# The second norm's scale and shift move behind the transposes, two token tiles at a time

## The chip, the core and the metric

The kernel runs on one core of a Trainium2 chip. Its engines are TensorE (PE in the rows, with its weight loads as PEld), VectorE (DVE), ScalarE (ACT) and GpSimd (POOL); SyncE (SP) issues most of the DMAs. The metric is the device time of one execution in microseconds (us), as the median of several timed runs.

## What is computed

One diffusion layer: 512 latent tokens and 256 context tokens of 1024 channels go through a mixer (linear attention and a state-space branch), and the latent tokens then through a feed-forward network. The change touches the place between the two:

```python
h_lat = h_lat + g1 * mix
h_lat = h_lat + g2 * _swiglu(modulate(rms_norm(h_lat, norm2_w), sh2, sc2), w_gate, w_up, w_down)

def rms_norm(x, w):        # y * w with y = x * rsqrt(mean(x*x) + EPS)
def modulate(h, shift, scale):
    return h * (1 + scale) + shift
```

`sh1, sc1, g1, sh2, sc2, g2` are the six parts of `silu(c) @ w_ada + b_ada`, so `sc2`, `sh2` and `norm2_w` hold one number for each channel and are the same for all tokens.

## The kernel before

All matrices are float32 and are multiplied in three passes: every operand is split into a high half (a rounded copy, made by ACT, line L188) and a low half (the rest, made by DVE or POOL, L189), and PE adds high x high, high x low and low x high (`mm3`, L204 to L206, for the row projections; L1067 to L1069 in the feed-forward network). Weights come in blocks of 512 KB through three `raw` buffers (L176, issued by SP) and are split into two buffers `whi` and two `wlo`.

Around the change the program runs as follows. The gates of the modulation (`ada`, a column for each of 48 blocks of 128 channels) are done while the mixer runs. Then `ada` is transposed, written to DRAM as rows (`adr`), and read back, spread over all 128 partitions: `g1r` (512 KB), `sh2` and `sc2` (two halves of 256 KB each) and `norm2_w` (`n2`, two halves), L949 to L963. DVE makes `sc2 = (1 + sc2) * n2` (L965).

Then comes the output projection. `merge(j)`, j from 0 to 7 (L980 to L991), loads two gate tiles `tgm_j_0` and `tgm_j_1` (and a third, `yam_j`, for j below 2) from DRAM into four buffers with the tag `E4`, and makes rows j of the operand on DVE (L988), POOL (L989), ACT (L990, high half) and DVE (L991, low half); each of these steps sets a buffer free for the loads of a later merge. The eight weight blocks `out_k` are multiplied with `g1r` on POOL (L187) and split. PE works through k = 0 to 3 for all tokens and then finishes k = 4 to 7 for one token tile `i` (128 tokens) after the other into the banks `ob[i][c]`.

For each token tile DVE adds the bank to `hres[i]` (L1022), ACT sums the squares (L1024), DVE and POOL make the factor `r` (L1027, L168, L170), and then

```python
nc.vector.scalar_tensor_tensor(xn, hres[i][...], r, sc2[half], ALU.mult, ALU.mult)     # L1031
(nc.gpsimd if (i, half) == (2, 1) else nc.vector).tensor_tensor(xn, xn, sh2[half], ALU.add)  # L1032
# L1035: four PE transposes of 128x128 into one PSUM bank
nc.scalar.activation(h2H[dst], pv, AF.Copy)                                            # L1038
nc.vector.tensor_tensor(h2L[dst], pv, h2H[dst].bitcast(F32), ALU.subtract)             # L1039
```

The feed-forward network begins with the weight blocks `gate` and `up` of j = 0 and 1 over tokens 0 to 255, then over tokens 256 to 511, so it needs tiles 0 and 1 first. From j = 2 on, `some_ada()` loads and sums one block of `w_ada` on POOL (L341 to L345) for the last gate `g2`, at every second j, eight blocks in all.

The order on each engine is set by a scheduler that plays the program on a timeline of its own; every engine then runs its list strictly in that order. Lines marked `tc.high_priority()` are put ahead.

## Time and profile before

| | |
|---|---|
| median of 3 runs | 1432.5 us (1431.48 to 1433.24) |
| the profiled execution's own time | 1428.55 us |
| its span from first to last instruction | 1426.7 us |
| busy PE, DVE, ACT, POOL | 95%, 62%, 35%, 33% of the span |
| DMA over the span | 175.49 MB moved, mean 123 GB/s |

The span is what the rows below are counted in; times in them are from its start. A busy share is a mean over stages with different limits, so the rows of single stretches tell more than the table. An idle time of an engine costs only where the work that ends last waits for it.

### The profile page before, as it was taken

Reading aid. Unit: us, or ns where it says so; the run is one execution under the profiler, and the core shown is the slowest. Engines: PE = TensorE matmul, PEld = TensorE weight load, DVE = VectorE, ACT = ScalarE, POOL = GpSimd, SP = SyncE. Lnnn points to the kernel's source line nnn. Section 1 sums busy time; section 2 is a strip of 40 time slices with the busy share of each in tenths; the row PEclk is TensorE's granted clock in tenths of the full one; section 3 lists DMA queues with packets and bytes.
Section 4 is the critical chain, followed back from the end, with each engine's and each line's share of the span. In section 5 each row is a group of like instructions: output and inputs, shape, how many; then the busy total and the mean of one; then the engine's idle time right before and its main releaser. Section 6 shows DMA issues by size and latency. Waiting matters only on the chain.

```text
span 1426.7 us, 19130 instructions
## 1 busy us (share of the span) xinstructions
PE 1349.4 (95%) x7462; PEld 1146.0 (80%) x7462; DVE 881.1 (62%) x1317; ACT 496.7 (35%) x825; POOL 476.1 (33%) x341
## 2 busy tenths in 40 slices
PE   5888999999998999998999989999889999999997
PEld 3687999889888778876887787778678888888886
DVE  4599757583595588558857975767683343433235
ACT  6464343433434132532332342332333323232222
POOL 1346555245423533343353324114641122100001
PEclk9998999999999999999999999999999999999999
DMA  9375433423422423323322333457423343333331
GB/s 370 123 259 151 128 102 111 126 93 126 122 75 67 141 98 101 97 73 90 104 82 89 96 97 101 158 184 267 135 87 109 113 122 115 120 116 93 100 106 72
DMA packets 71386, 175.49 MB, mean 123 GB/s; under 512 B 6384, under 2 KB 22912, under 8 KB 71168
## 3 DMA queue, kind: packets, MB, share of 16 engines
q1 hardware_dynamic: 57056, 161.11, 34.6%
q0 software_dynamic: 13952, 12.79, 3.8%
q8 instruction: 59, 0.97, 0.3%
q10 hardware_dynamic: 288, 0.36, 0.1%
...
## 4 chain that ended last, share of the span: by engine, by line
PE 66%; DVE 16%; DMA 9%; issue 5%; ACT 2%; POOL 1%; SPq 0%; POOLq 0%; DVEq 0%; ACTq 0%
DMA E<-cdr 6%; PE up L1069 3%; PE gate L1068 3%; PE gate L1069 3%; PE up L1068 3%; PE gate L1067 3%; PE up L1067 3%; DVE E L830 3%; PE db L204 3%; PE db L206 3%; PE db L205 3%; PE lv L577 2%; PE pb_pb L716 2%; PE pb_pb L715 2%; PE pb_pb L717 2%
## 5 line engine op out<-in xcount | busy, mean ns | idle before, releaser
L341 POOL TENSOR_TENSOR raw_ada<-raw_ada,cs 128x1024 f32<-128x1024 f32 x32 | 69.7, 2180 | 265.3 <-DMA raw_ada<-in_wts_dram 230.4
L830 DVE TENSOR_TENSOR E<-E,ebias 128x512 f32<-128x512 f32 x64 | 68.8, 1077 | 51.0 <-DMA E<-cdr 50.8
L343 POOL TENSOR_TENSOR raw_ada<-raw_ada 128x512 f32<-128x512 f32 x64 | 80.0, 1250 | 3.7
L386 PE MATMUL r_z<-whi_z,hH 128*128 128x256 f32 x256 | 74.6, 291 | 5.8 <-DVE z L781 3.0
L388 PE MATMUL r_z<-whi_z,hL 128*128 128x256 f32 x256 | 73.4, 287 | 0.0
L387 PE MATMUL r_z<-wlo_z,hH 128*128 128x256 f32 x256 | 73.0, 285 | 0.0
L1067 PE MATMUL gate<-h2H,whi_gate 128*128 128x512 f32 (+1 forms) x192 | 72.2, 376 | 0.0
L1068 PE MATMUL gate<-h2L,whi_gate 128*128 128x512 f32 (+1 forms) x192 | 72.1, 376 | 0.0
L1069 PE MATMUL gate<-h2H,wlo_gate 128*128 128x512 f32 (+1 forms) x192 | 71.9, 374 | 0.0
L189 POOL TENSOR_TENSOR wlo_xs<-raw_xs,whi_xs 128x1024 fp32r<-128x1024 f32 x16 | 40.6, 2536 | 75.3 <-ACT whi_xs L188 75.3
L1069 PE MATMUL up<-h2H,wlo_up 128*128 128x512 f32 x160 | 63.0, 394 | 0.0
L1068 PE MATMUL up<-h2L,whi_up 128*128 128x512 f32 x160 | 62.4, 390 | 0.0
L1067 PE MATMUL up<-h2H,whi_up 128*128 128x512 f32 x160 | 62.3, 389 | 0.0
L189 DVE TENSOR_TENSOR wlo_down<-raw_down,whi_down 128x1024 fp32r<-128x1024 f32 x18 | 22.1, 1225 | 62.4 <-ACT whi_down L188 62.3
L189 DVE TENSOR_TENSOR wlo_gate<-raw_gate,whi_gate 128x1024 fp32r<-128x1024 f32 x20 | 31.7, 1584 | 45.6 <-ACT whi_gate L188 45.6
L170 POOL TENSOR_TENSOR rr_f<-rv_f,negh 128x1 f32<-128x1 f32 x4 | 2.6, 662 | 168.5 <-DVE rv_f L168 168.5
L386 PE MATMUL r_v<-whi_v,hH 128*128 128x256 f32 x192 | 56.4, 294 | 0.0
L189 POOL TENSOR_TENSOR wlo_z<-raw_z,whi_z 128x1024 fp32r<-128x1024 f32 x16 | 39.6, 2475 | 49.2 <-ACT whi_z L188 36.6
L387 PE MATMUL r_v<-wlo_v,hH 128*128 128x256 f32 x192 | 55.5, 289 | 0.0
L715 PE MATMUL pb_pb<-yT,whi_pb 128*128 128x512 f32 x128 | 55.3, 434 | 0.0
L388 PE MATMUL r_v<-whi_v,hL 128*128 128x256 f32 x192 | 55.3, 288 | 0.0
L205 PE MATMUL db<-wlo_down,fH 128*128 128x512 f32 x142 | 55.3, 389 | 0.0
...
## 6 DMA issues: line engine op xcount, KB each, us to landing
...
```

Of the source, the lines that this page charges most:

```text
L189: (nc.gpsimd if split_pool[0] else nc.vector).tensor_tensor(lo, raw, hi.bitcast(F32), ALU.subtract)
L205: nc.tensor.matmul(out_, aH, bL, start=False, stop=False)
L341: nc.gpsimd.tensor_tensor(raw, raw, cs[:, :, 0:1].to_broadcast([P, KD, P]), ALU.mult)
L343: nc.gpsimd.tensor_tensor(raw[:, 0:n, :], raw[:, 0:n, :], raw[:, n:2 * n, :], ALU.add)
L386: nc.tensor.matmul(o, hH[:, kk, tk], hi[:, k, :], start=st, stop=False, skip_group_check=True)
L387: nc.tensor.matmul(o, hH[:, kk, tk], lo[:, k, :], start=False, stop=False, skip_group_check=True)
L388: nc.tensor.matmul(o, hL[:, kk, tk], hi[:, k, :], start=False, stop=sp, skip_group_check=True)
L715: nc.tensor.matmul(pt, hi[:, k, cl], aH[:, k, :], start=(k == 0), stop=False)
L830: nc.vector.tensor_tensor(ed, ed, ebias[:, d, n, hh].unsqueeze(2).to_broadcast([P, EH, P]), ALU.add)
L1067: nc.tensor.matmul(pts[kj][:, tk], hi[:, k, :], h2H[:, k, tk], start=(k == 0), stop=False)
L1068: nc.tensor.matmul(pts[kj][:, tk], hi[:, k, :], h2L[:, k, tk], start=False, stop=False)
L1069: nc.tensor.matmul(pts[kj][:, tk], lo[:, k, :], h2H[:, k, tk], start=False, stop=(k == KD - 1))
```

## The change

The scale and shift of the second norm are no longer rows spread over the partitions but columns, one number for each partition, used after the transposes, where the channels lie on partitions. The transposes therefore take `hres * r` alone, which ACT makes instead of DVE. Each PSUM bank now holds two blocks of 128 channels for two neighbouring token tiles, so that high and low halves are made for 256 tokens of one channel block at a time. The loads of `sh2`, `sc2` and `n2` and the two DVE steps on them are dropped, and only `g1` is written to DRAM. The last gate's blocks begin at j = 5 instead of 2.

```diff
-    adT = ch.tile([96, P], F32, tag="s2", name="adT", bufs=7)
+    adT = ch.tile([16, P], F32, tag="s2", name="adT", bufs=7)
...
-    sh2 = half_rows("sh2", 24)
-    sc2 = half_rows("sc2", 32)
-    for c in range(2):
-        n2 = ch.tile([P, 512], F32, tag="s2", name=f"n2_{c}", bufs=7)
-        nc.sync.dma_start(n2, rows[0:1, R_N2 + c * 512:R_N2 + (c + 1) * 512].to_broadcast([P, 512]))
-        nc.vector.scalar_tensor_tensor(sc2[c], sc2[c], 1.0, n2, ALU.add, ALU.mult)
+    s2c = cst.tile([P, KD], F32, name="s2c")
+    nc.vector.scalar_tensor_tensor(s2c, ada[:, 32:40, 0], 1.0, vecs[:, V_N2:V_N2 + KD], ALU.add, ALU.mult)
...
+        if i % 2 == 0:
+            pts = [sm_bank(f"hT_{i}_{q}") for q in range(4)]
         for half in range(2):
             xn = ch.tile([P, 512], F32, tag="z", name=f"hn_{i}_{half}", bufs=4)
-            nc.vector.scalar_tensor_tensor(xn, hres[i][:, half * 512:(half + 1) * 512], r, sc2[half], ALU.mult, ALU.mult)
-            (nc.gpsimd if (i, half) == (2, 1) else nc.vector).tensor_tensor(xn, xn, sh2[half], ALU.add)
-            pt = sm_bank(f"hT_{i}_{half}")
+            nc.scalar.activation(xn, hres[i][:, half * 512:(half + 1) * 512], AF.Copy, scale=r)
             for k in range(4):
-                nc.tensor.transpose(pt[:, k * P:(k + 1) * P], xn[:, k * P:(k + 1) * P], ident)
-            nc.scalar.activation(h2H[dst], pv, AF.Copy)
-            nc.vector.tensor_tensor(h2L[dst], pv, h2H[dst].bitcast(F32), ALU.subtract)
+                kk = half * 4 + k
+                c0 = (kk % 2) * 256 + (i % 2) * P
+                nc.tensor.transpose(pts[kk // 2][:, c0:c0 + P], xn[:, k * P:(k + 1) * P], ident)
+        if i % 2 == 1:
+            tk = slice((i - 1) * P, (i + 1) * P)
+            for k in range(KD):
+                pv = pts[k // 2][:, (k % 2) * 256:(k % 2) * 256 + 256]
+                sc, sh = s2c[:, k:k + 1], ada[:, 24 + k, 0:1]
+                nc.scalar.activation(h2H[:, k, tk], pv, AF.Identity, bias=sh, scale=sc)
+                hv = ch.tile([P, 256], F32, tag="s2", name=f"h2_{i}_{k}", bufs=7)
+                nc.vector.tensor_scalar(hv, pv, sc, sh, ALU.mult, ALU.add)
+                nc.vector.tensor_tensor(h2L[:, k, tk], hv, h2H[:, k, tk].bitcast(F32), ALU.subtract)
...
-        if j0 >= 2:
+        if j0 >= 5:
             some_ada()
```

The scheduler also moves work that the diff doesn't name. The first place is DVE's list in the output projection: `tgm_j_1` is the second gate tile of merge j (L988 before, L975 after), `mt` and `mL` are low halves of merged rows (L991 before, L978 after), `wlo_out_k` the low half of weight block k. Before:

```order
L189 TENSOR_TENSOR wlo_out_0_8944<-raw_out_0_8945,whi_out_0_8943 128x1024
L965 SCALAR_TENSOR_TENSOR sc2_0_8701<-sc2_0_8701,n2_0_8705 128x512
L965 SCALAR_TENSOR_TENSOR sc2_1_8703<-sc2_1_8703,n2_1_8708 128x512
L721 TENSOR_TENSOR acc_b_4899<-acc_b_4899,pb_pb_3_3_0_8891 128x512
L988 SCALAR_TENSOR_TENSOR tgm_2_1_8806<-tgm_2_1_8806,acc_b_4899 128x512
L721 TENSOR_TENSOR acc_b_4899<-acc_b_4899,pb_pb_3_3_1_8913 128x512
L189 TENSOR_TENSOR wlo_out_1_8975<-raw_out_1_8976,whi_out_1_8974 128x1024
L988 SCALAR_TENSOR_TENSOR tgm_3_1_8828<-tgm_3_1_8828,acc_b_4899 128x512
L991 SCALAR_TENSOR_TENSOR mt_1_8724<-tgm_2_0_8805,mt_0_8723 128x512
L988 SCALAR_TENSOR_TENSOR tgm_4_1_8856<-tgm_4_1_8856,acc_b_4899 128x512
L189 TENSOR_TENSOR wlo_out_2_9006<-raw_out_2_9007,whi_out_2_9005 128x1024
```

After, from the same place:

```order
L975 SCALAR_TENSOR_TENSOR tgm_2_1_8794<-tgm_2_1_8794,acc_b_4899 128x512
L721 TENSOR_TENSOR acc_b_4899<-acc_b_4899,pb_pb_3_2_1_8851 128x512
L189 TENSOR_TENSOR wlo_out_0_8932<-raw_out_0_8933,whi_out_0_8931 128x1024
L975 SCALAR_TENSOR_TENSOR tgm_3_1_8816<-tgm_3_1_8816,acc_b_4899 128x512
L721 TENSOR_TENSOR acc_b_4899<-acc_b_4899,pb_pb_3_3_0_8879 128x512
L978 SCALAR_TENSOR_TENSOR mt_1_8712<-tgm_2_0_8793,mt_0_8711 128x512
L189 TENSOR_TENSOR wlo_out_1_8963<-raw_out_1_8964,whi_out_1_8962 128x1024
L975 SCALAR_TENSOR_TENSOR tgm_4_1_8844<-tgm_4_1_8844,acc_b_4899 128x512
L978 SCALAR_TENSOR_TENSOR mt_1_8712<-tgm_3_0_8815,mt_0_8711 128x512
L978 SCALAR_TENSOR_TENSOR mL_0_8713<-tgm_4_0_8843,mt_0_8711 128x512
L975 SCALAR_TENSOR_TENSOR tgm_5_1_8866<-tgm_5_1_8866,acc_b_4899 128x512
L189 TENSOR_TENSOR wlo_out_2_8994<-raw_out_2_8995,whi_out_2_8993 128x1024
```

The merges now stand about one further ahead of the weight blocks: `wlo_out_2` had merge 4's L988 just ahead of it and now has merge 5's, with the low halves of merges 3 and 4. The same shift holds further down.

The second place is ACT's list at the norm: `w_up` and `whi_gate_1` are the high halves of the first feed-forward weights, `o_i_c` the sums of squares, `hn_i_half` the operand of the transposes, `hT` a bank with transposes. After:

```order
L188 ACTIVATE w_up_9351<-raw_up_1_9368 128x1024
L1021 ACTIVATE hn_0_0_9123<-hres_0_8703,rr_h0_9117 128x512
L1021 ACTIVATE hn_0_1_9129<-hres_0_8703,rr_h0_9117 128x512
L1011 ACTIVATE o_1_0_9161,hss_1_9159<-hres_1_8704 128x512
L1011 ACTIVATE o_1_1_9164,hss_1_9159<-hres_1_8704 128x512
L1021 ACTIVATE hn_1_0_9172<-hres_1_8704,rr_h1_9170 128x512
L1021 ACTIVATE hn_1_1_9178<-hres_1_8704,rr_h1_9170 128x512
L1011 ACTIVATE o_2_0_9242,hss_2_9240<-hres_2_8705 128x512
L1011 ACTIVATE o_2_1_9245,hss_2_9240<-hres_2_8705 128x512
L1021 ACTIVATE hn_2_0_9257<-hres_2_8705,rr_h2_9251 128x512
L188 ACTIVATE whi_gate_1_9362<-raw_gate_1_9364 128x1024
L1031 ACTIVATE h2H_9080<-hT_0_0_9119,ada_86,s2c_8697 128x256
```

Before, the same list had only the sums of squares of tile 1 between `w_up` and `whi_gate_1`, and the first `h2H` right behind. Now six `hn` and the sums of squares of tile 2 stand there.

The third place is PE's list at the start of the feed-forward network, after the last row of the output projection:

```order
L1062 MATMUL gate_0_9381<-h2H_9080,whi_gate_0_9352 128x256
L1062 MATMUL up_0_9382<-h2H_9080,w_up_9351 128x256
L1062 MATMUL gate_1_9383<-h2H_9080,whi_gate_1_9362 128x256
L1062 MATMUL up_1_9384<-h2H_9080,w_up_9351 128x256
L1063 MATMUL gate_0_9381<-h2L_9081,whi_gate_0_9352 128x256
...
L1062 MATMUL up_1_9384<-h2H_9080,w_up_9351 128x256
L1025 MATMUL hT_2_0_9253<-idt_77,hn_2_0_9257 128x128 x2
L1025 MATMUL hT_2_0_9253<-idt_77,hn_3_0_9306 128x128 x2
L1063 MATMUL gate_0_9381<-h2L_9081,whi_gate_0_9352 128x256
```

The transposes of tiles 0 and 1 now stand ahead of the output projection's last rows; before, those of tile 1 stood behind them. The first transposes of tiles 2 and 3 come after 16 feed-forward products; before, tile 2's came after some 40.

## Rows read from the trace of the kernel before

**Rows 1.** Timeline of PE, output projection: start, us, engine, line, [idle before <-releaser]

```profile
1007.04 0.50 PE L205 MATMUL ob<-wlo_out,mt 128*128 128x512 f32 x1 [2.41 <-DVE wlo_out L189]
...
1019.60 2.11 PE L204 MATMUL ob<-whi_out,mt 128*128 128x512 f32 x8 [0.80 <-ACT whi_out L188]
...
1022.64 0.50 PE L205 MATMUL ob<-wlo_out,mt 128*128 128x512 f32 x1 [0.94 <-DVE wlo_out L189]
...
1027.13 1.88 PE L204 MATMUL ob<-whi_out,mt 128*128 128x512 f32 x7 [0.57 <-ACT whi_out L188]
...
1031.73 0.50 PE L204 MATMUL ob<-w,mt 128*128 128x512 f32 x1 [1.36 <-ACT w L188]
```

**Rows 2.** Timeline of PE, from the projection's end to the feed-forward network

```profile
1050.98 1.97 PE L1035 MATMUL hT<-idt,hn 128*128 128x128 f32 x8 [4.68 <-DVE hn L1032]
...
1054.05 0.58 PE L1068 MATMUL gate<-h2L,whi_gate 128*128 128x256 f32 x1
```

**Rows 3.** Busy time by stretch: PE, PEld, DVE, ACT, POOL, PEclk, DMA share, GB/s

```profile
980.00:990.00 10.00, 10.00 (x46) 8.29 (x45) 8.07 (x7) 2.76 (x3) 7.24 (x3) 1.00 1.05 338
...
1005.00:1010.00 5.00, 2.96 (x10) 2.41 (x11) 4.38 (x4) 1.58 (x2) 2.16 (x2) 0.86 0.38 124
1010.00:1015.00 5.00, 4.98 (x18) 3.67 (x18) 2.01 (x3) 0.00 (x0) 3.56 (x2) 0.80 0.47 154
...
1050.00:1055.00 5.00, 3.98 (x16) 3.45 (x17) 4.93 (x11) 2.42 (x6) 0.87 (x2) 0.50 0.22 86
...
1300.00:1350.00 50.00, 50.00 (x222) 41.42 (x222) 12.34 (x12) 10.31 (x11) 0.00 (x0) 1.00 0.30 95
```

**Rows 4.** Timeline of SP's DMA issues, 978 to 985 us

```profile
978.40 1.64 SPq L955 DMA_DIRECT2D sh<-adr  x2
...
982.92 1.31 SPq L963 DMA_DIRECT2D n<-in_rows_dram  x2
984.33 0.53 SPq L982 DMA_DIRECT2D tgm<-tdr  x1
```

**Rows 5.** Timeline of DVE, output projection

```profile
996.12 2.88 DVE L988 SCALAR_TENSOR_TENSOR tgm<-tgm,acc_b 128x512 f32<-128x512 f32 x1
...
1004.58 1.28 DVE L988 SCALAR_TENSOR_TENSOR tgm<-tgm,acc_b 128x512 f32<-128x512 f32 x1 [2.76 <-DMA tgm<-tdr]
1005.78 1.21 DVE L189 TENSOR_TENSOR wlo_out<-raw_out,whi_out 128x1024 fp32r<-128x1024 f32 x1
```

**Rows 6.** Timelines of POOL and DVE at the norm, where both work at once

```profile
1040.48 2.61 POOL L189 TENSOR_TENSOR w_up<-raw_up,w_up 128x1024 fp32r<-128x1024 f32 x1 [1.09 <-ACT w_up L188]
...
1046.17 2.35 POOL L189 TENSOR_TENSOR wlo_gate<-raw_gate,whi_gate 128x1024 fp32r<-128x1024 f32 x1
...
1040.76 0.68 DVE L1022 TENSOR_TENSOR hres<-hres,ob 128x512 f32<-128x512 f32 x1
...
1046.24 3.49 DVE L1031 SCALAR_TENSOR_TENSOR hn<-hres,rr_h,sc 128x512 f32<-128x512 f32 x2 [0.66 <-POOL rr_h L170]
```

**Rows 7.** Timeline of ACT at the norm

```profile
1039.34 1.06 ACT L188 ACTIVATE w_up<-raw_up 128x1024 fp32r<-128x1024 f32 x1 [3.40 <-DMA raw_up<-in_wts_dram]
```

**Rows 8.** Groups by line and shape: count | busy us, mean ns | idle before

```profile
L1039 DVE TENSOR_TENSOR h2L<-hT,h2H 128x512 fp32r<-128x512 f32 x8 | 5.4, 681 | 0.8 <-ACT h2H L1038 0.8
...
L1038 ACT ACTIVATE h2H<-hT 128x512 fp32r<-128x512 f32 x8 | 4.8, 596 | 15.1 <-PE hT L1035 15.1
...
L170 POOL TENSOR_TENSOR rr_h<-rv_h,negh 128x1 f32<-128x1 f32 x4 | 2.2, 551 | 9.2 <-DVE rv_h L168 9.2
...
L740 ACT ACTIVATE cv_x<-c_xs,vecs 128x256 f32<-128x256 f32 x16 | 8.9, 554 | 0.0
...
L300 DVE TENSOR_SCALAR xnT<-xnT,s,ada 128x256 f32<-128x256 f32 x8 | 3.3, 410 | 0.0
...
L1134 DVE TENSOR_TENSOR hres<-hres,fnr 128x256 f32<-128x256 f32 x1 | 0.4, 426 | 0.6 <-ACT fo L1132 0.6
```

**Rows 9.** One line's instructions: duration in ns as min/median/max

```profile
L1146 ACT ACTIVATE fin<-hres,rr_f x1: 722/722/722, 1422.7 to 1422.7; 128x512 f32<-128x512 f32 x1
```

More of the change, by code (lines that the diff above doesn't have):

```diff
@@ L39 @@
 V_TOT = 200
-R_GN, R_DS, R_DTB, R_AL, R_SN, R_FN, R_N2 = 0, 256, 288, 352, 416, 2464, 3488
-R_TOT = 4512
+R_GN, R_DS, R_DTB, R_AL, R_SN, R_FN = 0, 256, 288, 352, 416, 2464
+R_TOT = 3488
 M_ID, M_LE, M_GE, M_GT, M_LT, M_ONE = range(6)
@@ L941, in hybrid_layer_kernel @@
     pt = sm_bank("adaT")
-    nc.tensor.transpose(pt[0:96, 0:P], ada.rearrange("p j t -> p (j t)"), ident)
-    adT = ch.tile([96, P], F32, tag="s2", name="adT", bufs=7)
-    nc.vector.tensor_copy(adT, pt[0:96, 0:P])
-    adr = dr.tile([96, P], F32, name="adr")
+    nc.tensor.transpose(pt[0:16, 0:P], ada[:, 16:24, :].rearrange("p j t -> p (j t)"), ident)
+    adT = ch.tile([16, P], F32, tag="s2", name="adT", bufs=7)
+    nc.vector.tensor_copy(adT, pt[0:16, 0:P])
+    adr = dr.tile([16, P], F32, name="adr")
     nc.gpsimd.dma_start(adr, adT)
-    arow = adr.rearrange("(j t) p -> t j p", t=2)
     g1r = pj.tile([P, D], F32, tag="p4", name="g1r")
-    nc.sync.dma_start(g1r.rearrange("p (j c) -> p j c", c=P), arow[0:1, 16:24, :].to_broadcast([P, 8, P]))
-    def half_rows(name, j0):
-        ts = []
-        for c in range(2):
-            t = ch.tile([P, 512], F32, tag="s2", name=f"{name}_{c}", bufs=7)
-            nc.sync.dma_start(t.rearrange("p (j c) -> p j c", c=P), arow[0:1, j0 + 4 * c:j0 + 4 * c + 4, :].to_broadcast([P, 4, P]))
-            ts.append(t)
-        return ts
-    sh2 = half_rows("sh2", 24)
-    sc2 = half_rows("sc2", 32)
-    for c in range(2):
-        n2 = ch.tile([P, 512], F32, tag="s2", name=f"n2_{c}", bufs=7)
-        nc.sync.dma_start(n2, rows[0:1, R_N2 + c * 512:R_N2 + (c + 1) * 512].to_broadcast([P, 512]))
-        nc.vector.scalar_tensor_tensor(sc2[c], sc2[c], 1.0, n2, ALU.add, ALU.mult)
+    nc.sync.dma_start(g1r.rearrange("p (j c) -> p j c", c=P),
+                      adr.rearrange("(j t) p -> t j p", t=2)[0:1].to_broadcast([P, 8, P]))
+    s2c = cst.tile([P, KD], F32, name="s2c")
+    nc.vector.scalar_tensor_tensor(s2c, ada[:, 32:40, 0], 1.0, vecs[:, V_N2:V_N2 + KD], ALU.add, ALU.mult)
     hp.close()
@@ L1028, in hybrid_layer_kernel @@
             r = rstd_of(ss, D, f"h{i}")
+        if i % 2 == 0:
+            pts = [sm_bank(f"hT_{i}_{q}") for q in range(4)]
         for half in range(2):
             xn = ch.tile([P, 512], F32, tag="z", name=f"hn_{i}_{half}", bufs=4)
-            nc.vector.scalar_tensor_tensor(xn, hres[i][:, half * 512:(half + 1) * 512], r, sc2[half], ALU.mult, ALU.mult)
-            (nc.gpsimd if (i, half) == (2, 1) else nc.vector).tensor_tensor(xn, xn, sh2[half], ALU.add)
-            pt = sm_bank(f"hT_{i}_{half}")
+            nc.scalar.activation(xn, hres[i][:, half * 512:(half + 1) * 512], AF.Copy, scale=r)
             for k in range(4):
-                nc.tensor.transpose(pt[:, k * P:(k + 1) * P], xn[:, k * P:(k + 1) * P], ident)
-            dst = (slice(None), slice(half * 4, half * 4 + 4), slice(i * P, (i + 1) * P))
-            pv = pt.rearrange("p (k t) -> p k t", t=P)
-            nc.scalar.activation(h2H[dst], pv, AF.Copy)
-            nc.vector.tensor_tensor(h2L[dst], pv, h2H[dst].bitcast(F32), ALU.subtract)
+                kk = half * 4 + k
[10 more added lines that the diff above has]
+                nc.vector.tensor_tensor(h2L[:, k, tk], hv, h2H[:, k, tk].bitcast(F32), ALU.subtract)
     tc.keep_in_program_order(nc.scalar.preload_act_table_set("silu_and_others"))
@@ L1187, in lay_out @@
         a["gla_norm_w"][0], a["d_skip"][0], a["dt_bias_f"][0], a["dt_bias_b"][0], a["a_log_f"][0], a["a_log_b"][0],
-        a["ssm_norm_w"][0], a["final_norm_w"], a["norm2_w"][0]]).reshape(1, R_TOT)
+        a["ssm_norm_w"][0], a["final_norm_w"]]).reshape(1, R_TOT)
     up = np.zeros((96, 2, 512), f32)
```

## The prediction

> **What bounds the kernel now.** I read the busy time by stretch first, to see where TensorE is the limit. In the feed-forward network PE is busy 50.00 of 50 us with 222 products [rows 3], 0.225 us for each: nothing that DVE, ACT or POOL saves there can shorten it, unless PE is made to wait. So I looked in PE's timeline for the places where it does wait and the change touches something. There are two. In the output projection PE stands idle 2.41, 0.80, 0.94, 0.57 and 1.36 us, each time for the high or low half of a weight block [rows 1], and just behind the first stall it also runs below full clock: 0.86 of it over 1005 to 1010 and 0.80 over 1010 to 1015 [rows 3], a loss of 5 × 0.14 + 5 × 0.20 = 1.7 us. Between projection and network it waits 4.68 us for `hn` of tile 1, which DVE makes (L1031, L1032), and the first product with `h2L` stands at 1054.05 [rows 2]; over 1050 to 1055 the granted clock is 0.50, the 1.2 GHz level [rows 3].
>
> Behind these waits stand DVE and the loads. The first stall's `wlo_out_2` ran at 1005.78, directly behind a merge step that had waited 2.76 us for its `tgm` [rows 5]. DVE is also slow when POOL works: the same merge step takes 1.28 us or 2.88 [rows 5], and the two L1031 at 1046.24 take 3.49 us while POOL is at `wlo_gate` from 1046.17 [rows 6].
>
> **The change, part by part.**
>
> *The dropped loads.* Six loads of 256 KB (512 columns × 4 bytes × 128 partitions), 1.57 MB. SP issues them from 978.40 to 984.2, and the next `tgm` is issued only behind them, at 984.33 [rows 4]; over 980 to 990 the DMA engines are full (share 1.05, 338 GB/s [rows 3]), so that these bytes alone are 1.57 / 0.338 = 4.65 us of all engines. The merges' loads can therefore come up to about 5 us earlier, and DVE loses two L965. A merge is a chain (load, DVE, POOL, ACT, DVE) that sets its buffers free only at its end, so the earliness arrives thinned. The order shows what it meets: each merge now stands about one further ahead of the weight blocks on DVE.
>
> (A) The four later stalls, 0.80 + 0.94 + 0.57 + 1.36 = 3.67 us [rows 1], are waits for splits of `out_4` to `out_7` that stood behind merges 5 to 7. With merges one ahead and their loads earlier I take all four as gone: −3.67, bounds 0 and −3.67.
>
> (B) The stall at `wlo_out_2` with its clock loss is 2.41 + 1.7 = 4.1 us. This block now waits behind merge 5 instead of merge 4, and the lists put two low halves ahead of it; the loads are earlier, the list is longer. Bounds 0 and −4.1; as neither row decides, half: −2.0.
>
> These 5.7 us also move what follows: the `raw` buffers of the feed-forward weights come free by the very splits for which PE waits here, so I take `w_up_1` (1039.34, 3.40 us idle for its load [rows 7]) and all behind it as moved along, and count (C) on the old times.
>
> (C) *The norm.* Before, DVE made `hn` in four slow steps for a tile; now ACT makes it, in two. ACT's 128x512 steps last 0.60 from a bank and 0.72 with a scale for each partition [rows 8, 9]; I take 0.65. The order on ACT fixes the chain: `w_up_1` at 1039.34 [rows 7] ends at 1040.4; two `hn_0` to 1041.6; two `o_1` to 1042.9; the factor (two small DVE steps, then `rr_h` with 0.55 on POOL [rows 8]) to 1044.5; two `hn_1` to 1045.9; two `o_2` to 1047.2; the factor of tile 2 to 1048.1; two `hn_2` to 1049.5; only then `whi_gate_1`, 1.06 like `w_up` [rows 7], to 1050.5, and the first `h2H` (0.55, as L740 [rows 8]) to 1051.05. So what DVE had been late with, ACT's order is late with now. Then POOL begins `wlo_gate_1` at 1050.6 and needs 2.35 to 2.4 [rows 6]. The new `h2L` is a DVE subtraction with both inputs in SBUF, like L1031 at 1046.24; the old one had an input in PSUM and lasted 0.68 in all eight [rows 8]. If POOL holds it, `h2L` ends at 1053.0 + 0.43 (the 128x256 subtraction of L1134 [rows 8]), and the first product that needs it begins at about 1053.5 against 1054.05: −0.6. If it isn't held, the chain is 1051.05 + 0.41 + 0.43, at about 1051.9: −2.1. And if PE, waiting less, also keeps its clock there, up to 3.0 us more: (1.00 − 0.50) × 5 = 2.5 for the stretch of 1050 to 1055 [rows 3], and 0.5 for one us more at that level, an estimate. −5.1 is the outer bound. I take −0.6.
>
> The row for this choice: DVE's L1022, with one input in PSUM, took 0.68 at 1040.76 in the middle of POOL's 1040.48 to 1043.09, but L1031, both inputs in SBUF, 3.49 for two [rows 6]. The Trainium skill, "SBUF — State Buffer", section "Who interferes with whom", gives the rule: a DVE instruction that reads two inputs from SBUF contends with GpSimd, one that reads a single SBUF input doesn't, as the port is an exclusive lock. It speaks against the new `h2L`, and these rows agree with it; by it (C) is −0.6, without it −2.1.
>
> *ACT's and DVE's totals.* ACT gains eight steps of 0.72 [rows 9] and sixteen of 0.55 for eight of 0.60 [rows 8]: 14.7 for 4.8 us. DVE gets sixteen pairs of 0.41 + 0.43 [rows 8] for its L1031, L1032, L1039 and L965, and is relieved. Both lie beside PE's work but for chain (C). For tiles 2 and 3 the cover is the sixteen products ahead of their transposes and the rest of the first 256 tokens: 96 products of 256 columns, half of 0.225 each, 10.8 us, against some 3 us of ACT for `hn_3` and eight `h2H`; nothing taken. `s2c` is one step of 128x8 under the mixer: nothing; uncovered under 0.41 [rows 8].
>
> *The last gate.* Its blocks move out of 1054 to 1063, where POOL's sums stand between tile 2's and 3's factors; PE is the bound until the `down` blocks, and eight blocks at every second j from 5 end before those. Nothing, either way.
>
> *Sum.* −3.67 − 2.0 − 0.6 = −6.3. On the profiled execution's 1428.55 that is 1422.3. It stands 4 us under the median of 1432.5, so I subtract from the median: 1426.2.
>
> **The rivals.**
>
> *All of it, PE never waits* (15%). The earlier loads bring `wlo_out_2` in time, its stall and the clock loss go, and `h2L` isn't held: −3.67 − 4.1 − 5.1 = −12.9, 1419.6. For it: DMA is full only to about 990 [rows 3], and DVE loses two steps there. Against it: `wlo_out_2` stands behind one more merge, and ACT's list puts `whi_gate_1` behind six `hn`.
>
> *The change doesn't do it* (20%). The merges are paced by their own chain of buffers, not by the dropped loads: `tgm` was late again at 1004.58, twenty us after SP's queue had become free [rows 5]. Then stalls (A) and (B) only move to other blocks and (C) gives −0.6 to −1: 1431.5, no change that can be told. A difference under 0.2%, 2.9 us, can't be told from none here.
>
> *Slower: DVE held in the merges* (10%). DVE's list has more merge steps with two SBUF inputs ahead of `wlo_out_2`, and they now come when POOL adds and scales. Six of them at 2.88 [rows 5] instead of 0.68 (the unheld duration of L1022 [rows 6]) are 13.2 us more, and if two such holds, 4.4, are in the old times already, `wlo_out_2` comes 8.8 later, at 1014.6, and PE's first stall grows by as much. With (A) and (C) that is +8.8 − 3.67 − 0.6 = +4.5: 1437.0. It decides from `wlo_out_2` later than about 1010 (1005.78 + 3.67 + 0.6), less what the earlier loads give back, up to 5.
>
> **How the numbers follow.** The likeliest has 55%: faster by 6.3 us, its own range 1422 to 1429.5 (A at half, B at 0 to −4.1). The range holds it, most of the second rival and half of the first: 1420.5 to 1432.0. Faster by more than 0.2% are the likeliest and the first rival, 70%; within it the second, 19%; slower the third and what else may be late, 11%.
>
> **What the profile would show.** For (A): the later stalls of PE's rows before the norm gone, the DMA share over 980 to 990 well under 1.05. For (B): `wlo_out_2` at 1003 to 1006 with less than 2.41 idle before its first product. For (C): the first product with `h2L` less than a microsecond earlier against the projection's end than before, ACT idle only for the factors, the first `h2L` on DVE ending with POOL's `wlo_gate_1` and longer than 0.43; the clock still 0.50 in that stretch. I am wrong if PE's stalls sit where they were (second rival), if `h2L` doesn't wait for POOL, or if a transposed tile 2 or 3 keeps PE waiting inside the network.

## The result and the profile after

The changed kernel is slower: 1443.15 us in the median of 9 runs (1435.45 to 1445.77) against 1431.74 (1425.35 to 1436.41) in 9 runs of the kernel before, a ratio of 1.0063 [1.0043, 1.0083], with its 95% interval; the quotient of the two medians, 1.0080, lies inside it. The forecast was 1426.2. The profiled execution took 1435.45 us (a span of 1433.7), 6.9 more than before's 1428.55.

To see where, I cut both traces at four products of PE that both kernels have: the first of the output projection, the first of 512 columns in the feed-forward network (all the tokens; the ones ahead of it are 256 wide), the first of the `down` blocks (`db`), and the end of the last.

| stage (us) | before | after | difference |
|---|---|---|---|
| up to the output projection | 992.2 | 992.8 | +0.6 |
| projection and norm, to the first 512-wide product | 87.2 | 86.5 | −0.7 |
| 512-wide `gate` and `up` products | 219.7 | 225.8 | +6.1 |
| `down` blocks | 115.8 | 116.4 | +0.6 |
| tail | 11.8 | 12.3 | +0.4 |

The loss stands where the diff changes nothing, and where PE is never idle. The first row says little: that stage lies between 992 and 1004 us in the traces of this document. Busy time by stretch of the changed kernel, as in [rows 3] (PE, PEld, DVE, ACT, POOL, PEclk, DMA share, GB/s):

```profile
980.00:990.00 10.00, 10.00 (x46) 8.28 (x45) 7.98 (x7) 2.76 (x3) 6.73 (x3) 1.00 0.93 304
1005.00:1010.00 5.00, 2.92 (x14) 2.09 (x12) 3.76 (x4) 0.81 (x1) 3.46 (x2) 1.00 0.46 145
1010.00:1015.00 5.00, 4.65 (x19) 3.58 (x20) 4.70 (x3) 2.21 (x3) 3.75 (x3) 1.00 0.65 193
1050.00:1055.00 5.00, 2.48 (x10) 2.19 (x11) 3.02 (x6) 4.45 (x11) 2.89 (x2) 0.50 0.12 22
1100.00:1150.00 50.00, 50.00 (x217) 40.31 (x216) 19.62 (x20) 14.49 (x18) 10.50 (x8) 1.00 0.37 115
```

The last of these stretches in the kernel before:

```profile
1100.00:1150.00 50.00, 50.00 (x225) 41.48 (x224) 20.34 (x21) 14.45 (x18) 12.09 (x11) 1.00 0.42 131
```

Over 1100 to 1150 PE is busy 50.00 of 50 us, at full clock, in either kernel. Before, this window holds 225 products; now 217. A busy engine at the same clock does less: each product takes longer. The duration of one instruction shows it (min/median/max in ns). Before:

```profile
L1067 PE MATMUL up<-h2H,whi_up x160: 388/389/390, 1084.9 to 1298.5; 128*128 128x512 f32 x160
L204 PE MATMUL db<-whi_down,fH x142: 388/390/390, 1299.1 to 1392.3; 128*128 128x512 f32 x142
L204 PE MATMUL db<-whH,fH x28: 388/389/390, 1393.0 to 1414.1; 128*128 128x512 f32 x28
```

After:

```profile
L1062 PE MATMUL up<-h2H,whi_up x160: 392/395/396, 1084.8 to 1304.3; 128*128 128x512 f32 x160
L204 PE MATMUL db<-whi_down,fH x142: 389/389/395, 1305.0 to 1398.2; 128*128 128x512 f32 x142
L204 PE MATMUL db<-whH,fH x28: 392/396/397, 1398.9 to 1420.5; 128*128 128x512 f32 x28
```

`up` and the last `down` products went from 389 to 395 and 396 ns; the other `down` products, of the same shape, stayed at 389 to 390. From one start to the next, the 960 products of 512 columns take 226.8 ns before and 233.3 now, 6.2 us in all. What the two slow groups share and the third lacks is where their operands lie in SBUF. The kernel allocates from both ends: `whi_*`, `wlo_*`, `fH` and most else on the low side, `h2H`, `h2L`, `hH`, `hres` and the pair `whH`, `whL` (weights of the last `down` blocks) on the high side (pool `top`, with a filler of 120 columns, `top_pad`). The tile addresses of the two built programs, in bytes within a partition:

| tile | side | before | after |
|---|---|---|---|
| `whi_gate_0` | low | 32768 | 32800 |
| `fH` | low | 61696 | 61728 |
| `h2H` | high | 196096 | 196096 |
| `h2L` | high | 212480 | 212480 |

`s2c` is 8 columns of 4 bytes, allocated in the low pool `cst` ahead of the weights: it moves all that is allocated later on that side by 32 bytes. `up` multiplies a low with a high tile, so the distance of its two operands changes, and so does that of the last `down` products (`whH` high, `fH` low); `db` with `whi_down` has both on the low side.

In the projection PE's waits did not go away. Its timeline (idle time before, and its releaser), to be set beside [rows 1, 2]:

```profile
997.21 0.50 PE L204 MATMUL ob<-whi_out,mt 128*128 128x512 f32 x1 [0.17 <-DVE acc_b L721]
...
999.18 0.50 PE L204 MATMUL ob<-whi_out,mt 128*128 128x512 f32 x1 [1.00 <-DVE acc_b L721]
...
1001.90 0.50 PE L205 MATMUL ob<-wlo_out,mt 128*128 128x512 f32 x1 [0.63 <-DVE wlo_out L189]
...
1009.98 0.50 PE L205 MATMUL ob<-wlo_out,mt 128*128 128x512 f32 x1 [2.08 <-DVE wlo_out L189]
...
1014.71 1.67 PE L204 MATMUL ob<-whi_out,mt 128*128 128x512 f32 x6 [0.35 <-ACT whi_out L188]
...
1017.74 0.50 PE L205 MATMUL ob<-wlo_out,mt 128*128 128x512 f32 x1 [1.36 <-DVE wlo_out L189]
...
1031.71 0.50 PE L204 MATMUL ob<-w,mt 128*128 128x512 f32 x1 [1.66 <-ACT w L188]
...
1051.47 0.58 PE L1062 MATMUL gate<-h2H,whi_gate 128*128 128x256 f32 x1 [3.59 <-ACT h2H L1031]
...
1053.74 0.58 PE L1063 MATMUL gate<-h2L,whi_gate 128*128 128x256 f32 x1 [1.05 <-DVE h2L L1034]
```

There are seven stalls of 7.25 us together in the projection, where [rows 1] have five of 6.08.

My theory after this: three independent terms, the place of `s2c` (some +7), the new norm (a gain), and the dropped loads, which reorder the lists. The rival: the 32 bytes matter only through something else that the change does, such as transfers or steps that now run beside the network.

### The profile page after: what moved, and what is told of

It is laid out like the page before. It is cut to its first block, busy times and chain, and to the rows that moved or that the text cites. A ratio compares the mean times of both kernels' runs of the same rounds, so it can differ in the third digit from the quotient of the medians.

```text
span 1433.7 us, 19151 instructions
## 1 busy us (share of the span) xinstructions
PE 1356.9 (95%) x7462; PEld 1142.0 (80%) x7462; DVE 870.6 (61%) x1325; ACT 505.5 (35%) x841; POOL 475.3 (33%) x340
## 4 chain that ended last, share of the span: by engine, by line
PE 69%; DVE 15%; DMA 7%; issue 4%; ACT 2%; POOL 2%; SPq 0%; POOLq 0%; DVEq 0%; ACTq 0%
DMA E<-cdr 5%; PE up L1064 3%; PE gate L1063 3%; PE gate L1064 3%; PE up L1063 3%; PE gate L1062 3%; PE up L1062 3%; PE db L205 3%; PE db L204 3%; PE db L206 3%; DVE E L830 2%; PE pb_pb L715 2%; PE pb_pb L716 2%; PE pb_pb L717 2%; PE lv L577 2%
## 5 line engine op out<-in xcount | busy, mean ns | idle before, releaser
L833 ACT ACTIVATE E<-E 128x512 f32<-128x512 f32 x32 | 20.2, 631 | 101.3 <-DVE E L832 80.8
L206 PE MATMUL db<-whi_down,fL 128*128 128x512 f32 x142 | 55.3, 389 | 0.0
L386 PEld LDWEIGHTS r_z<-whi_z,hH 128*128 128x128 f32 x256 | 49.5, 193 | 7.1 <-issue 4.2
```

The source lines that it names most:

```text
L206: nc.tensor.matmul(out_, aL, bH, start=False, stop=stop)
L386: nc.tensor.matmul(o, hH[:, kk, tk], hi[:, k, :], start=st, stop=False, skip_group_check=True)
```

## The experiments

All ratios are to the kernel before, with a 95% interval; the runs were made on several chips, so the ratios compare and the medians don't. The last four columns are read from one trace of each kernel: the stages above (norm: from the end of the projection's last product to the first 512-wide one, a part of the column before it).

| run | median us | ratio | projection + norm | norm | 512-wide | `down` |
|---|---|---|---|---|---|---|
| before | 1431.74 | | 87.2 | 33.1 | 219.7 | 115.8 |
| changed | 1443.15 | 1.0063 [1.0043, 1.0083] | 86.5 | 31.4 | 225.8 | 116.4 |
| e1_s2c_top | 1432.70 | 0.9999 [0.9980, 1.0017] | 89.2 | 32.2 | 219.7 | 115.8 |
| e2_before_pad32 | 1440.55 | 1.0049 [1.0032, 1.0065] | 87.8 | 33.8 | 225.8 | 116.4 |
| e3_before_pad64 | 1439.70 | 1.0035 [1.0018, 1.0052] | 86.8 | 31.8 | 225.9 | 116.3 |
| e4_after_pad64 | 1441.92 | 1.0045 [1.0026, 1.0064] | 86.8 | 31.8 | 225.9 | 116.3 |
| e5_both32 | 1433.31 | 1.0006 [0.9989, 1.0024] | 87.7 | 32.5 | 219.7 | 115.8 |
| e6_no_row_loads | 1432.28 | 1.0001 [0.9982, 1.0021] | 86.0 | 31.7 | 219.7 | 115.8 |
| e7_split32 | 1434.43 | 1.0015 [1.0000, 1.0030] | 87.3 | 32.1 | 219.7 | 115.8 |
| e8_norm_alone | 1428.42 | 0.9977 [0.9958, 0.9996] | 83.4 | 28.3 | 219.7 | 115.8 |
| e8_again | 1428.01 | 0.9973 [0.9958, 0.9987] | 84.0 | 29.1 | 219.7 | 115.8 |
| e9_gate1_dve | 1436.25 | 1.0018 [0.9998, 1.0037] | 88.1 | 31.6 | 219.7 | 115.8 |
| e10_hn2_dve | 1435.25 | 1.0010 [0.9989, 1.0030] | 88.9 | 31.6 | 219.7 | 115.8 |
| e11_both_dve | 1432.82 | 0.9992 [0.9974, 1.0010] | 87.1 | 31.3 | 219.7 | 115.8 |
| e12_norm_late_gate | 1428.63 | 0.9979 [0.9962, 0.9995] | 84.5 | 28.7 | 219.7 | 115.8 |
| e14_norm_shifted | 1437.33 | 1.0044 [1.0026, 1.0061] | 84.9 | 29.0 | 225.8 | 116.4 |

Small steps in the norm column are not the kernels' alone, as PE's clock enters it: e2_before_pad32 and e3_before_pad64 differ in the width of a pad alone and have 33.8 and 31.8, with 3.4 and 1.7 us of lost clock there ((1 − PEclk) × 5 us, summed over stretches of 5 us).

### The 32 bytes: e1_s2c_top and e2_before_pad32

The one takes the shift out of the changed kernel, the other puts nothing but the shift into the kernel before.

```diff
-    top.tile([P, 120], F32, name="top_pad")       # e1_s2c_top, from the changed kernel
+    top.tile([P, 112], F32, name="top_pad")
-    s2c = cst.tile([P, KD], F32, name="s2c")
+    s2c = top.tile([P, KD], F32, name="s2c")
...
+    cst.tile([P, 8], F32, name="end_pad")         # e2_before_pad32, from the kernel before
```

> The change with its one new constant tile s2c (32 bytes a partition) taken out of an existing pad at the other end of SBUF, so that every other tile lies where it lay before the change. Theory A (where the weights lie against the activations sets PE's pace: 0.227 us a product before, 0.232 to 0.2335 after in the feed-forward network): the 128x512 products of the network take 0.389 to 0.390 again, the stage from its first 512-wide product to the down blocks is back at 214 us instead of 220, and the time is that of before or up to 3 us less, ratio 0.998 to 1.000. Theory B (the norm, the new order of the engines or the moved last gate cost the time): ratio about 1.006 as the change. Theory C (PE's pace differs from run to run): a mixture, and both paces appear in kernels of either layout.

> The kernel before with nothing but an unused tile of 32 bytes a partition at the end of the pool of constants, which moves all later tiles of the low side by 32 bytes. Theory A: slower like the change, ratio 1.005 to 1.007 (960 products of the network by 5.5 ns, 5.3 us, the last down products 1 us, and the projections of the mixer either way), with 0.395 in the network. Theory B: ratio 1.000. Theory C: no steady difference.

The 512-wide stage fell back to 219.7 in the first and rose to 225.8 in the second, though its pad is never read or written. (The expectation has 214 and 220 for this stage; the traces have other values, but the same step of 6.) One instruction's durations, of e1_s2c_top:

```profile
L1062 PE MATMUL up<-h2H,whi_up x160: 389/389/389, 1092.9 to 1306.4; 128*128 128x512 f32 x160
```

and of e2_before_pad32:

```profile
L1068 PE MATMUL up<-h2H,whi_up x160: 392/395/396, 1090.0 to 1309.5; 128*128 128x512 f32 x160
```

So the address alone does it, and the rival (transfers or steps beside the network) falls. It also follows that all else in the change together was worth nothing that can be told: 0.9999.

### How far a shift must go: e3_before_pad64 and e4_after_pad64

```diff
+    cst.tile([P, 16], F32, name="end_pad")                       # e3_before_pad64
...
-    s2c = cst.tile([P, KD], F32, name="s2c")                     # e4_after_pad64
+    s2c = cst.tile([P, 2 * KD], F32, name="s2c")[:, 0:KD]
```

> The kernel before with an unused tile of 64 bytes at the same place. Theory A with a period of 64 bytes: ratio 1.000, products at 0.389. Theory A with a longer period, or any other move of the weights: some other pace, ratio 1.003 to 1.008. Theory B: 1.000.

> The change with s2c made 64 bytes a partition wide, half of it unused, so that the low side moves by 64 bytes instead of 32. Theory A with a period of 64 bytes: as the change with s2c out of the way, ratio 0.998 to 1.000 of before. With a longer period: 1.003 to 1.008. Theory B: 1.006, as the change.

A period of 64 bytes was wrong: both kept the slow pace, 225.9. A durations row of e4_after_pad64:

```profile
L1062 PE MATMUL up<-h2H,whi_up x160: 393/394/398, 1091.8 to 1311.4; 128*128 128x512 f32 x160
```

### PE alone: m1_offsets

The layer is left out, and the kernel ran once. PE multiplies two constant operands; one is moved away from the other in steps, first with 24 products of 512 columns at each distance (`wide`, where the operand that streams through PE is moved), then with 24 of 256 (`rows_`, where the one that PE holds is moved).

```diff
+    W = sb.tile([P, 2048], F32R, name="W")
...
+    X = sb.tile([P, 8192 + 2048], F32R, name="X")
...
+    steps = [0, 16] + list(range(32, 512, 32)) + [512, 544, 768, 1024, 1536, 2048, 4096]
+    for d in steps:
+        wide(f"o{d}b", d)
```

> PE alone: groups of 24 products in the network's order (eight k of high x high, high x low, low x high; nothing else of the layer is computed), the stationary blocks fixed, the moving operand d bytes further along the partition, d = 0, 16, 32, then every 32 to 480, and 512, 544, 768, 1024, 1536, 2048, 4096; then 16 groups of 256 columns, in which the moved tile is the stationary one; at last d = 0, 32, 64, 256 again. d = 0 is the place of before. If the two operands' places against each other alone set the pace: 0.227 us a product at d = 0, 0.232 to 0.2335 at -32 or 32, about 0.2335 at 64, the same numbers in the repeats, and 0.227 at d = 256 (the output projection of before has the operands 256 apart and runs at 0.227); multiples of 512 like d = 0. If other engines' traffic in the layer is needed for it: 0.227 or one other pace in all groups.

PE's timeline shows the first product of each group (the name has the distance in bytes, counted from a place where the two operands lie a multiple of 256 bytes apart), so that the pace is the time to the next group by 24:

```profile
44.68 0.39 PE L152 MATMUL o0b<-X,W 128*128 128x512 f32 x1
...
50.12 0.39 PE L152 MATMUL o16b<-X,W 128*128 128x512 f32 x1
...
55.68 0.40 PE L152 MATMUL o32b<-X,W 128*128 128x512 f32 x1
...
61.28 0.39 PE L152 MATMUL o64b<-X,W 128*128 128x512 f32 x1
...
66.78 0.40 PE L152 MATMUL o96b<-X,W 128*128 128x512 f32 x1
...
94.81 0.39 PE L152 MATMUL o256b<-X,W 128*128 128x512 f32 x1
...
100.27 0.40 PE L152 MATMUL o288b<-X,W 128*128 128x512 f32 x1
```

At distance 0 it is (50.12 − 44.68) / 24 = 226.7 ns; at 32, 233.3; at 64, 229.2; at 256, 227.5. By the starts in whole ns, from the first to the last product of each group (23 steps):

| distance, bytes | 0 | 16 | 32 | 64 | 96 | 128 | 160 | 192 | 224 | 256 | 288 | 320 | 1024 |
|---|---|---|---|---|---|---|---|---|---|---|---|---|---|
| 512 wide, ns | 226.7 | 231.4 | 233.5 | 228.7 | 233.9 | 233.5 | 234.0 | 233.5 | 233.1 | 227.7 | 233.4 | 229.3 | 226.7 |
| 256 wide, ns | 119.7 | | 118.3 | 117.8 | 117.3 | 118.3 | 120.1 | 117.8 | 117.9 | 119.6 | | | |

Repeats at 0, 32, 64 and 256 gave 228.7, 233.5, 229.3 and 227.7, so that 64 can't be told from 0 here. So the pace depends on the distance modulo 256 and not only on whether it is a multiple of 32 or 64; the expectation of 233.5 at 64 was wrong here. It is not wrong in the layer: there the low tile moves up by 64, which is a distance of −64, or 192, and 233.5. The changed kernel's shift is −32, or 224: 233.1. In the kernel before, the operands of all 512-wide products of weights lie at 0 (addresses of the built program), the least value found, so no other layout promises more for these. The 256-wide products go the other way by 1.4 to 2.4 ns, but for the distance of 160 (120.1). In the layer, the network's 192 products of 256 columns, whose weights PE holds as in `wide`, took 119.8 ns from start to start before, 118.3 in the changed kernel and 113.7 in e3_before_pad64.

### Both sides moved: e5_both32 and e7_split32

```diff
-    top.tile([P, 120], F32, name="top_pad")       # e5_both32, from the changed kernel
+    top.tile([P, 112], F32, name="top_pad")
...
+    hpool.tile([P, 8], F32, name="hp_pad")        # e7_split32: e5_both32 and this
```

> The change with its 32 bytes of s2c on the low side as they are, and the pad at the other end of SBUF 32 bytes smaller, so that the activations on that side move by 32 bytes too: the operands lie against each other as in before, but each 32 bytes off its old address. If the places against each other set the pace: 0.389 in the network, 219.7 us from its first 512-wide product to the down blocks, ratio 0.998 to 1.001. If an operand's own address does (a multiple of 64 or more): 0.395, 225.8 us, ratio 1.005.

> As the run with both sides moved, but the mixer's activations stay at their old address, 32 bytes off against the weights, where the 256-wide products run at 0.117 us in place of 0.120 and the 512-wide ones at up to 0.2335 in place of 0.227. Network at 0.227, 219.7 us. The mixer: 1488 products less 3 ns, -4.5 us, 384 of the gate projections plus 6.5 ns, +2.5, some 576 others plus 2 to 4 ns, +1.5: about -0.5 us against the run with both sides moved, ratio 0.998 to 1.001.

With `s2c` where the change puts it, and the high side moved as far, the distance is as before and so is the pace. Durations in e5_both32:

```profile
L1062 PE MATMUL up<-h2H,whi_up x160: 389/389/389, 1087.2 to 1300.7; 128*128 128x512 f32 x160
...
L204 PE MATMUL db<-whH,fH x28: 389/389/389, 1395.3 to 1416.3; 128*128 128x512 f32 x28
```

That it is the distance, and not an address by itself, is thereby shown. e7_split32 puts the pool with `hH` back to its old address, for a gain of some 0.5 us in the mixer by its narrow products: none can be told (1.0015 against 1.0006).

### The dropped loads alone: e6_no_row_loads

```diff
-    sh2 = half_rows("sh2", 24)
-    sc2 = half_rows("sc2", 32)
...
+    sh2 = sc2 = [g1r[:, 0:512], g1r[:, 512:1024]]
```

This is the kernel before without the six loads and L965; it leaves out the true shift and scale.

> The kernel before without the six row loads and without the two steps that make sc2; the norm's steps stay as they were but take a gate row in place of scale and shift, so that these values are left out. It has the merges' new order on DVE. By the prediction's terms (A) and (B), the stretch from the first product of the output projection to the network's first 512-wide one is 87.2 us less 3.7 to 5.7: 81.5 to 83.5, and the time 0.996 to 0.997 of before. If the merges are paced by DVE, which POOL holds up, or by their buffers: stalls in the first blocks in place of the later ones, 86 to 89 us, ratio 0.999 to 1.002.

1.0001: dropping the loads gave nothing by itself. PE's timeline in it:

```profile
1003.18 0.50 PE L204 MATMUL ob<-whi_out,mt 128*128 128x512 f32 x1 [0.16 <-DVE acc_b L721]
...
1005.14 0.50 PE L204 MATMUL ob<-whi_out,mt 128*128 128x512 f32 x1 [0.98 <-DVE acc_b L721]
...
1007.86 0.50 PE L205 MATMUL ob<-wlo_out,mt 128*128 128x512 f32 x1 [0.62 <-DVE wlo_out L189]
...
1037.72 0.50 PE L204 MATMUL ob<-w,mt 128*128 128x512 f32 x1 [1.64 <-ACT w L188]
```

0.16, 0.98, 0.62 and 1.64 are the changed kernel's 0.17, 1.00, 0.63 and 1.66, with the old norm. The new pattern of stalls therefore comes from dropping the loads alone.

### The norm alone: e8_norm_alone, e8_again and e12_norm_late_gate

```diff
+    s2c = top.tile([P, KD], F32, name="s2c")      # from the kernel before, loads and L965 kept
+    nc.vector.scalar_tensor_tensor(s2c, ada[:, 32:40, 0], 1.0, vecs[:, V_N2:V_N2 + KD], ALU.add, ALU.mult)
...
-        if j0 >= 2:                               # e12_norm_late_gate alone
+        if j0 >= 5:
```

> The new norm alone: s2c in the pad of the other side, all addresses as before, the last gate's blocks from j = 2, and the six row loads and the two steps on them kept (their result is not used). If the dropped loads alone moved the merges and with them PE's stalls: the output projection has the stalls of before again (2.4, 0.8, 0.9, 0.6, 1.4 us) and none at the accumulators in its first blocks. The norm by term (C): from the projection's end to the network's first 512-wide product 0.6 to 2 us less than the 33.1 of before. Ratio 0.998 to 1.001. If the norm's steps on ACT move the merges: the stalls of the change.

> The new norm alone once more, row loads kept, s2c out of the way, last gate from j = 2. If its gain is real: ratio 0.996 to 0.999, PE's waits at the norm under 2 us in all against 4.7 before, no lowered clock there. If it was the spread between executions: 0.999 to 1.001.

> The same with the last gate's blocks from j = 5. If the dropped row loads take the norm's gain away: as the norm alone, 0.996 to 0.999, since the gate's place changes no list ahead of j = 2. If the later gate does: 0.999 to 1.002, with the network from j = 2 longer than 219.7 us or a wait at the down blocks.

The norm is that of the changed kernel, and `top_pad` has 112 columns, so that no address moves. The loads and L965 run but their results aren't used. These are the only kernels whose interval lies below the one before: 0.9977, 0.9973, and 0.9979 with the last gate's place as well. The gain is in the norm stage, 28.3 to 29.1 us against 33.1, which is more than the 0.6 to 2 us expected of term (C). The stalls of the projection are those of before, as expected, and one more of 1.64 us at `out_3` that wasn't.

Two things make the gain in the norm. PE's waits there add up to 2.26, 1.97 and 1.78 us in the three traces, against 4.68 before. And its clock falls less: over 1045 to 1065 the clock lost is 3.4 us before, 1.7 in e8_again and e12_norm_late_gate, and 0 in e8_norm_alone, where the stretch that had 0.50 before reads

```profile
1050.00:1055.00 5.00, 3.25 (x21) 2.34 (x20) 2.55 (x5) 5.00 (x12) 2.92 (x2) 1.00 0.05 6
```

PE's timeline in e12_norm_late_gate at the start of the network:

```profile
1048.69 0.39 PE L1076 MATMUL gate<-h2H,whi_gate 128*128 128x256 f32 x1 [0.51 <-ACT h2H L1045]
...
1049.87 0.38 PE L1076 MATMUL up<-h2H,w_up 128*128 128x256 f32 x1 [0.56 <-DVE hres L1024]
...
1050.97 0.54 PE L1077 MATMUL gate<-h2L,whi_gate 128*128 128x256 f32 x1 [0.72 <-DVE h2L L1048]
```

and ACT's:

```profile
1047.15 1.04 ACT L188 ACTIVATE whi_gate<-raw_gate 128x1024 fp32r<-128x1024 f32 x1
1048.10 0.55 ACT L1045 ACTIVATE h2H<-hT,ada,s2c 128x256 fp32r<-128x256 f32 x1
1048.54 1.32 ACT L1035 ACTIVATE hn<-hres,rr_h 128x512 f32<-128x512 f32 x2
```

The wait for the first `h2H` is 0.51 instead of the changed kernel's 3.59. With the loads kept, the scheduler puts `whi_gate_1` and the first `h2H` ahead of `hn` of tile 2; in the changed kernel ACT did them in the other order:

```profile
1048.69 1.33 ACT L1021 ACTIVATE hn<-hres,rr_h 128x512 f32<-128x512 f32 x2 [1.04 <-POOL rr_h L170]
1049.93 1.04 ACT L188 ACTIVATE whi_gate<-raw_gate 128x1024 fp32r<-128x1024 f32 x1
1050.88 1.00 ACT L1031 ACTIVATE h2H<-hT,ada,s2c 128x256 fp32r<-128x256 f32 x2
```

### Is it that order? e9_gate1_dve, e10_hn2_dve, e11_both_dve

All three start from e1_s2c_top (loads dropped, address mended). The first makes `wlo_gate_1` on DVE, so that POOL can't hold `h2L`; the second takes `hn` of tile 2 off ACT's list; the third does both.

```diff
+        split_pool[0] = j == 0                    # e9, around the split of ("gate", j)
...
+            if i == 2:                            # e10
+                nc.vector.tensor_scalar(xn, hres[i][:, half * 512:(half + 1) * 512], r, None, ALU.mult)
+            else:
+                nc.scalar.activation(xn, hres[i][:, half * 512:(half + 1) * 512], AF.Copy, scale=r)
```

> The change with s2c out of the way and one more edit: the low half of the weight block gate_1 is made on DVE instead of POOL. If POOL holds DVE's first h2L (1.65 us in the change's run, against 0.42 of the last): the first h2L takes 0.42, but stands behind a weight split of 1.2 us; PE's wait for it goes from 1.5 to 0.5 to 1.5 us, the stage from the projection's end to the first 512-wide product from 32.2 to 31 to 32. If something else held it: 1.65 as it was, the stage 32 to 33. Ratio 0.998 to 1.001 either way.

> The change with s2c out of the way and the operand hn of token tile 2 made on DVE, so that ACT's list has whi_gate_1 and the first h2H directly behind the squares of tile 2. If ACT's list is what is late at the norm: PE's wait for the first h2H goes from 3.2 to 3.6 us to about 2, the stage from the projection's end to the first 512-wide product from 32.2 to about 31. If not: no change of that wait. Ratio 0.997 to 1.000.

> Both of the last two edits together. If ACT's list and POOL's hold are the two lateness of the norm: the stage from the projection's end to the first 512-wide product at 30 to 31 us, ratio 0.997 to 0.999. If the norm is bounded by something else: 32 us, 1.000.

None can be told from the kernel before. DVE's first `h2L`, in e9_gate1_dve:

```profile
1060.32 0.43 DVE L1034 TENSOR_TENSOR h2L<-h,h2H 128x256 fp32r<-128x256 f32 x1
```

It took 0.43 here against 1.65 in the changed kernel (below), so the hold is real; but the stage gained only 0.6 (31.6 against 32.2). In e10_hn2_dve the first wait for `h2H` fell from 3.2 to 0.80 us and the next one, for DVE's sum L1009, was 3.09. The first of the two `hn` had moved beside POOL's `wlo_gate_1` and took 2.62 us, the second, behind it, 0.47: groups by line (count | busy us, mean ns | idle before), of e10_hn2_dve

```profile
L1022 DVE TENSOR_SCALAR hn<-hres,rr_h 128x512 f32<-128x512 f32 x2 | 3.0, 1546 | 0.1
```

and of e11_both_dve, where POOL has no `wlo_gate_1`:

```profile
L1022 DVE TENSOR_SCALAR hn<-hres,rr_h 128x512 f32<-128x512 f32 x2 | 0.9, 484 | 0.1
```

With both, the norm stage is 31.3, still 2.2 to 3 above the kernels with the loads. PE still waits 3.30 us there: 1.22 for `h2H` and 2.09 for DVE's L1009, where e12_norm_late_gate waits 0.56 for the same sum; and the clock lost is 3.4 us again. So the order of `hn` of tile 2 and the hold of `h2L` are each a part of the chain, but removing them doesn't give the gain back. Why L1009 comes late in the reordered lists stays open.

### The address once more: e14_norm_shifted

```diff
-    top.tile([P, 112], F32, name="top_pad")       # from e12_norm_late_gate
+    top.tile([P, 120], F32, name="top_pad")
-    s2c = top.tile([P, KD], F32, name="s2c")
+    s2c = cst.tile([P, KD], F32, name="s2c")
```

> The last kernel with s2c on the low side, so that the weights lie 32 bytes off again. If the address cost is a term of its own: 6.7 us more than the last kernel (225.8 for 219.7 in the network, 116.4 for 115.8 in the down blocks), ratio 1.001 to 1.004 of before and 0.4 to 0.5% above the last kernel.

1.0044 against 0.9979, a quotient of 1.0065, somewhat more than the 0.4 to 0.5% expected: the address costs the same on top of the kernel with the gain, again +6.1 and +0.6 by stages.

## Why the prediction was wrong

**The step that failed** is "`s2c` is one step of 128x8 under the mixer: nothing". I costed the time of the step that fills it and not its place. The shift costs 0.5% to 0.65% (e2_before_pad32 1.0049; e14_norm_shifted against e12_norm_late_gate 1.0065): +6.1 us in the 512-wide stage and +0.6 in the `down` blocks. The sentence on [rows 3] that nothing can shorten the network "unless PE is made to wait" had the same hole: PE can run slower while it is busy all the time. The sum of −6.3 lacked this term. What the medians show beyond 6.7 us (0.65% is 9.3) no trace places. The sum failed without it too: with the address mended, e1_s2c_top has 0.9999, since (A) and (B), 5.7 of the 6.3, didn't come as forecast. The slower rival named DVE held in the merges; that was there, but small.

**(A), −3.67:** wrong; what failed is "I take all four as gone". By the program's order of products, the stalls at `out_4` and `out_5` went, but two of 0.35 and 1.36 came at `out_3`, and the last, at `out_6` and `out_7`, grew from 1.36 to 1.66: 3.37 in place of 3.67. New ones of 0.17, 1.00 and 0.63 came at `out_0` and `out_1`, so that the term is +1.5. The loads did come earlier, as forecast: `tgm` was issued at 979.83 instead of 984.33, and the DMA share over 980 to 990 fell from 1.05 to 0.93. But a merge one place further ahead in DVE's strict list stands in front of the sums (L721) that PE waits for. Before, the last two of them ran ahead of merge 3's step; now they run behind it. The list of the changed kernel shown with the change leaves out the very last, for `pb_pb_3_3_1`, between `mt` and `wlo_out_1`; it is the row at 998.45. DVE in the changed kernel:

```profile
993.68 2.88 DVE L975 SCALAR_TENSOR_TENSOR tgm<-tgm,acc_b 128x512 f32<-128x512 f32 x1
996.48 0.68 DVE L721 TENSOR_TENSOR acc_b<-acc_b,pb_pb 128x512 f32<-128x512 f32 x1
997.08 1.45 DVE L978 SCALAR_TENSOR_TENSOR mt<-tgm,mt 128x512 fp32r<-128x512 f32 x1
998.45 0.68 DVE L721 TENSOR_TENSOR acc_b<-acc_b,pb_pb 128x512 f32<-128x512 f32 x1
...
1008.71 1.21 DVE L189 TENSOR_TENSOR wlo_out<-raw_out,whi_out 128x1024 fp32r<-128x1024 f32 x1
...
1052.03 1.65 DVE L1034 TENSOR_TENSOR h2L<-h,h2H 128x256 fp32r<-128x256 f32 x1
```

and POOL:

```profile
992.63 3.38 POOL L187 TENSOR_TENSOR raw_out<-raw_out,g1r 128x1024 f32<-128x1024 f32 x1
...
1051.05 2.36 POOL L189 TENSOR_TENSOR wlo_gate<-raw_gate,whi_gate 128x1024 fp32r<-128x1024 f32 x1 [2.39 <-ACT whi_gate L188]
```

A merge step of 2.88 us beside POOL's product, and the two L721 queued behind it: those are PE's new waits of 0.17 and 1.00. This is the rival "the change doesn't do it", in its words "move to other blocks", and e6_no_row_loads shows it apart.

**(B), −2.0:** the number came out, by luck, and not by the mechanism. The stall is 2.08 instead of 2.41 and PEclk is 1.00 where it was 0.86 and 0.80, about −2. But the sign that the prediction named, `wlo_out_2` at 1003 to 1006, is not there: DVE made it at 1008.71, against 1005.78 before. PE came to it later too, after the new stalls of 1.80 us, and so waited less. And e5_both32 has the same lists and a stall of 2.12 us, and its window reads

```profile
1010.00:1015.00 5.00, 3.67 (x11) 2.90 (x12) 4.77 (x4) 1.23 (x3) 3.42 (x2) 0.75 0.49 154
```

so that the clock's part comes and goes: e12_norm_late_gate stalls 3.04 us at the same place and keeps 1.00.

**(C), −0.6:** right in mechanism, and in size at the old pace. There the norm stage is 32.2 and 32.5 (e1_s2c_top, e5_both32) against 33.1: −0.9 and −0.6. The chain over ACT was forecast to begin the first `h2H` at 1050.5 and did at 1050.88. `h2L` ended with POOL's `wlo_gate_1` (1053.68 against 1053.41) after 1.65 us, as the rule of the Trainium skill, "SBUF — State Buffer", section "Who interferes with whom", says of two SBUF inputs; the trace agrees, 0.43 where POOL was free. The other half of that rule, on a single SBUF input, the Trainium skill states only outside DVE's 2-port modes, a condition that the prediction left out. `hn` on DVE in e10_hn2_dve has one such input and took 2.62 us beside POOL; in which mode it ran, no run shows. The clock over 1050 to 1055 stayed 0.50. In the changed kernel the stage shows −1.8; its 192 products of 256 columns, 1.5 ns less each, make 0.3 of that, and the rest no run explains. The outer bound of −5.1 was not out of reach: with the loads kept the norm stage gained 4.0 to 4.8, by shorter waits and by the clock.

**The last gate, nothing:** right, 0.9979 against 0.9977 and 0.9973, and 219.7 in all.

**Against a page of the Trainium skill:** "TensorE: Matmul & The Clock Gate", section "Step-by-step: what each phase is for", has PE read its two operands by independent ports, so that loading the next weights takes nothing from the running product. By it one would expect the 32 bytes to cost nothing; m1_offsets shows 226.7 and 233.5 ns, a difference of 3%, with no other engine at work. The measurement decides. What in PE or SBUF collides at these distances no run here shows; it stays open. The mixer pays and is paid back: from start to start, its 512-wide products with `hH` and `hL` went from 229.9 to 233.3 ns and the 256-wide ones of the row projections from 122.7 to 120.1; e2_before_pad32 has 233.2 and 120.2, e7_split32 233.3 and 120.0. With some 770 and 1640 such steps in the trace that is about +2.6 and −4.3 us, an estimate.

**The better kernel.** The new norm with `s2c` out of the way and the row loads kept, e8_norm_alone, beats both in the ratio: 0.9977 [0.9958, 0.9996] and 0.9973 [0.9958, 0.9987].
